# One 1024-column tile per k-step for the modulation matmuls of a two-layer decoder step, and the first normalised input in two halves

## The chip, the cores and the metric

The kernel runs on one core of a Trainium2 chip. The metric is the device time of one execution in microseconds (us). Everything is float32; the weights of the large products are split into a high and a low part (fp32r) and multiplied in three passes.

## The reference, cut to what matters

A two-layer decoder step over 512 prompt tokens and 8 x 4 sample tokens, width 1024. Each layer has a mixer and a ConvFFN, and each of these is wrapped in RMSNorms whose shift, scale and gate come from a condition vector `c` by one product per layer:

```python
c_act = jax.nn.silu(c)                      # 1 prompt row + 8 sample rows = 9 rows of 1024
for l in range(DEPTH):
    mod = (c_act @ w["ada_w"][l] + w["ada_b"][l])[:, None, :]     # 1024 -> 6144
    sh1, sc1, g1, sh2, sc2, g2 = jnp.split(mod, 6, axis=-1)
    h = _rmsnorm(x, ng[0]) * (1 + sc1) + sh1
    y, ... = _mixer_ab(h, ...) if l % 2 == 0 else _mixer_cd(h, ...)
    x = x + g1 * _rmsnorm(y, ng[1])
    h = _rmsnorm(x, ng[2]) * (1 + sc2) + sh2
    y, ... = _conv_ffn(h, ...)
    x = x + g2 * _rmsnorm(y, ng[3])
```

`ada_w` is 2 x 1024 x 6144 in float32, 50 MB of the 208 MB that the kernel moves. It is used for nine rows only.

## The kernel before

Activations lie feature-major: 128 features on the partitions, 8 k-blocks, two halves `h` of 272 tokens (256 prompt, 16 sample). A large product (`gemm`, `mm`, L527 to L531) takes one 128-column block of weights at a time: per k-block three matmuls for each half, 272 columns each. Weights come in `wraw` tiles of 256 KB (`load_w`), ScalarE makes the high part (L510), VectorE or GpSimd the low part (L511).

The order of each engine's instructions is fixed when the kernel is built, by a planner that goes through the program in order, models the time of each instruction and puts on each engine's list whatever is ready by its model; an earlier line of the program goes first. On the chip an engine then keeps to its list. SyncE (SP) issues all DMAs, also in the order of its list, and waits there when the buffer of the next DMA isn't free.

**The modulation product.** `ada(l, s)` makes 2048 of the 6144 columns of layer `l`. Stationary is `cact`, 128 x 32 (nine columns of it used), so a matmul uses a quarter of TensorE's columns, and four of them go to the four quarters of one PSUM bank:

```python
for k in range(KB):
    for j in range(4):
        wt = ada_tile()                                   # 128 x 512, 256 KB
        SY.dma_start(wt, t["ada_w"][l, k, :, o:o + 512])
        PE.matmul(ps[32*j:32*j+32, :], cact[:, k, :], wt, start=(k == 0), stop=(k == KB - 1))
    yield
```

Then ScalarE copies the bank out (L407), four 128-column transposes turn it (L410), and VectorE adds the bias and makes `mod`, `cA` (scale) and `cG` (gate). There are six calls, so 48 k-steps, 192 DMAs and 192 matmuls. In the trace a float32 matmul has two records.

**Where it runs.** `ada(0,0)` is the prologue: nothing of the network can start before it. `ada(0,1)` and `ada(0,2)` are woven into mixer 0 and `ada(1,*)` into the first ConvFFN: after each block of the gemm `weave` steps a side generator, and `pace(7, 8)` or `slow(2)` sets how many blocks go by for one k-step. The tiles come from `wraw` (7 buffers) in the prologue, from a pool `st0` (6) in mixer 0, and from pools of 4 later.

**The first input.** In the prologue `xprep` squares the input X (L458), sums it over the features on TensorE (`rstd`, L442) and multiplies by the result (L1224); `first` applies scale and shift (L1233 to L1239) once `ada(0,0)` is complete. Half 0 and half of half 1 are prepared in the prologue, the rest in `second()`, after the first half of the three lead blocks of mixer 0's gemm.

Of the kernel before, what the change touches and what calls it, by code (L numbers as in the profile page):

```python
# [41 lines left out]
XRB = 6  # L42
# [225 lines left out]
def build(nc, tc, ctx, t):  # L268
# [14 lines left out]
    def psum1(name="p1"):  # L283
        return pp.tile([P, 512], F32, name=name, tag="p1", bufs=3)
# [5 lines left out]
    cst = cp.tile([P, NCST], F32, name="cst")  # L290
    cact = cp.tile([P, KB, 32], F32, name="cact")
# [97 lines left out]
    apool = []  # L389
# [7 lines left out]
    def ada(l, s):  # L397
        ps = psum1("psada")
        for k in range(KB):
            for j in range(4):  # L400
# [7 lines left out]
        pt = psum1("psadat")  # L408
# [3 lines left out]
        V.tensor_tensor(  # L412
            mods[l][:, s * 16:s * 16 + 16, :].rearrange("p (j c) n -> p j c n", c=4),
            pt.rearrange("p (c j n) -> p j c n", c=4, j=4)[:, :, :, 0:NMOD],
            par[:, o:o + 16].rearrange("p (j c) -> p j c", c=4).unsqueeze(3).to_broadcast([P, 4, 4, NMOD]),
            op=ADD)

        def ng(i):
            oo = PAR["norm_g"][0] + (l * 4 + i) * KB
            return par[:, oo:oo + KB].unsqueeze(2).to_broadcast([P, KB, NMOD])  # L420

        mb = mods[l]
        if s == 0:
            V.scalar_tensor_tensor(cA[l][0], mb[:, 8:16, :], 1.0, ng(0), op0=ADD, op1=M)
        elif s == 1:
            V.tensor_tensor(cG[l][0], mb[:, 16:24, :], ng(1), op=M)
        else:
            V.scalar_tensor_tensor(cA[l][1], mb[:, 32:40, :], 1.0, ng(2), op0=ADD, op1=M)
            V.tensor_tensor(cG[l][1], mb[:, 40:48, :], ng(3), op=M)
        yield  # L430
# [73 lines left out]
    def load_w(ap, kc, eng):  # L504
# [3 lines left out]
        n = kc * P  # L508
        SY.dma_start(raw[:, :n], ap.rearrange("p k n -> p (k n)"))
        A.activation(hi[:, :n], raw[:, :n], AF.Copy)  # L510
        eng.tensor_tensor(lo[:, :n], raw[:, :n], hi[:, :n], op=SUB)  # L511
        return hi, lo

    def load_block(w, n, k0, k1, eng):
        out = []
        for a in range(k0, k1, 4):
            b = min(a + 4, k1)
            hi, lo = load_w(w[n, :, a:b, :], b - a, eng[a // 4 % 2])
            out += [(hi[:, i * P:(i + 1) * P], lo[:, i * P:(i + 1) * P]) for i in range(b - a)]
        return out  # L520
# [97 lines left out]
    def ffn(l, nxt, side, pre):  # L618
# [11 lines left out]
        if l == 0:  # L630
            apool.append((fp, 4))
# [42 lines left out]
        def body():  # L674
# [10 lines left out]
            apool.clear()  # L685
# [8 lines left out]
    def mixer0(nxt, side, pre, loaded):  # L694
# [5 lines left out]
        apool.append((st0, XRB))  # L700
# [84 lines left out]
        apool[-1] = (es.enter_context(pool("mix0w")), 4)  # L785
# [5 lines left out]
        apool.clear()  # L791
# [398 lines left out]
    def bias_vectors():  # L1190

        rel = ada_tile()[0:64, 0:12]
        SY.dma_start(rel, t["rel"])
        for c in range(3):
            oh, rv = ada_tile()[0:64, :], ada_tile()[0:12, :]
# [17 lines left out]
    er = ExitStack()  # L1213
    st0 = er.enter_context(pool("mix0r", side="right"))
    XR = {}

    def xprep(h, c0, c1):

        if c0 == 0:
            XR[h] = rstd(squares(h), onesD)  # L1220
        r = XR[h].unsqueeze(1).to_broadcast([P, CH, HT])
        for c in range(c0, c1, CH):
            XR[h, c] = st0.tile([P, CH, HT], F32, name="xr", tag="adaw", bufs=XRB)
            V.tensor_tensor(XR[h, c], X[:, c:c + CH, h, :], r, op=M)  # L1224
# [16 lines left out]
    a = ada(0, 0)  # L1241
# [3 lines left out]
    steps(a, 1)  # L1245
    ao, io = PAR["a_w"][0], CST["flip"][0]
    SY.dma_start(par[:, :ao], t["par"][:, :ao])
    SY.dma_start(cst[:, :io], t["cst"][:, :io])
    steps(a, 1)
    xprep(0, 0, KB)  # L1250
    steps(a, 1)
    xprep(1, 0, CH * (XRB - 4))
# [35 lines left out]
```

## Time and profile before

| | us |
|---|---|
| median of 3 runs | 1499.38 (1497.99 to 1500.75) |
| the profiled execution | 1496.03 |
| its span | 1494.3 |
| TensorE busy | 1417.8 (95%) |
| VectorE / ScalarE / GpSimd busy | 882.1 / 618.8 / 170.6 |
| mean granted TensorE clock | 0.978 of full speed |

All times within the execution are counted from the start of the span. A granted clock of 1.00 is 2.4 GHz and 0.50 is 1.2 GHz; a value between them in a row is a mean over a stretch with both. What a stretch of TensorE work costs is read from start to start of neighbouring instructions, since the ends of pipelined matmuls are modelled and overlap the next start.

### The profile page before, as it was taken

How to read it: one execution, taken by the hardware profiler on the slowest of the kernel's cores; microseconds unless marked ns; L12 is line 12 of the kernel's file. 1: busy time of each engine (PE TensorE's matmuls, PEld its weight loads, DVE VectorE, ACT ScalarE, POOL GpSimd, SP SyncE). 2: the span in 40 equal slices, each digit the busy share in tenths (PEclk: the TensorE clock that was granted, in tenths of full speed). 3: DMA queues.
4: the chain of work that ended last, by engine and by line, in shares of the span. 5: the costliest groups of instructions: out<-in, count | busy, mean ns of one | idle time of the engine just before them, and what ended most of it. 6: DMA issues, size and time to landing. Idle time of an engine off the chain costs nothing.

```text
span 1494.3 us, 26853 instructions
## 1 busy us (share of the span) xinstructions
PE 1417.8 (95%) x10354; PEld 1271.0 (85%) x10354; DVE 882.1 (59%) x1788; ACT 618.8 (41%) x1145; POOL 170.6 (11%) x384
## 2 busy tenths in 40 slices
PE   6899997999999999999799999999699999999995
PEld 2578897988798798899699999678599999999995
DVE  1664427753165346446859979652886456456457
ACT  2322235743244234235652442643674444244244
POOL 0210014110011001001500000000521011011011
PEclk9799998999999999999999999999899999999998
DMA  7775633325445546544236245446122332332311
GB/s 264 242 253 187 201 106 100 103 98 180 160 155 194 161 139 212 165 158 186 89 113 197 94 141 178 135 146 239 57 85 69 103 93 71 104 91 65 113 51 61
DMA packets 112633, 207.72 MB, mean 139 GB/s; under 512 B 20884, under 2 KB 33684, under 8 KB 111992
## 3 DMA queue, kind: packets, MB, share of 16 engines
q1 hardware_dynamic: 112504, 206.00, 42.5%
q8 instruction: 81, 1.33, 0.4%
q14 instruction: 48, 0.39, 0.1%
HBM read 198.63 MB, written 34.39 MB: 156 GB/s over the span
## 4 chain that ended last, share of the span: by engine, by line
PE 88%; DVE 6%; DMA 2%; ACT 2%; issue 1%; SPq 0%; POOL 0%; POOLq 0%; DVEq 0%; ACTq 0%
PE psmm L527 23%; PE psmm L531 23%; PE psmm L529 23%; PE psada L404 6%; PE psn L442 2%; PE psmh L529 2%; PE psmh L527 2%; PE psmh L531 2%; PE pso L1013 1%; PE psl L979 1%; PE psl L981 1%; DVE X L492 1%; DVE Yf L491 1%; DVE Y L491 1%; DVE Hlo L481 1%
## 5 line engine op out<-in xcount | busy, mean ns | idle before, releaser
L510 ACT ACTIVATE whi<-wraw 128x512 fp32r<-128x512 f32 (+1 forms) x404 | 239.8, 600 | 511.4 <-PE psmm L529 411.6
L527 PE MATMUL psmm<-Hhi,whi 128*128 128x272 f32 x2028 | 435.9, 291 | 1.0 <-DVE extu L750 1.0
L531 PE MATMUL psmm<-Hhi,wlo 128*128 128x272 f32 x2028 | 431.4, 289 | 0.3 <-POOL wlo L511 0.3
L529 PE MATMUL psmm<-Hlo,whi 128*128 128x272 f32 x2028 | 430.0, 288 | 0.0
L511 DVE TENSOR_TENSOR wlo<-wraw,whi 128x512 fp32r<-128x512 f32 (+1 forms) x374 | 240.8, 649 | 303.4 <-ACT whi L510 288.3
L527 PEld LDWEIGHTS psmm<-Hhi,whi 128*128 128x128 f32 x2028 | 321.4, 189 | 24.3 <-issue 12.6
L529 PEld LDWEIGHTS psmm<-Hlo,whi 128*128 128x128 f32 x2028 | 322.5, 189 | 9.0 <-issue 9.0
L531 PEld LDWEIGHTS psmm<-Hhi,wlo 128*128 128x128 f32 x2028 | 321.5, 189 | 9.9 <-issue 9.2
L527 PE MATMUL psmm<-act_hi,whi 128*128 128x272 f32 x624 | 135.5, 290 | 0.0
L531 PE MATMUL psmm<-act_hi,wlo 128*128 128x272 f32 x624 | 135.3, 289 | 0.0
L529 PE MATMUL psmm<-act_lo,whi 128*128 128x272 f32 x624 | 132.7, 288 | 0.0
L578 DVE SCALAR_TENSOR_TENSOR fz<-fext,par,fz 128x560 f32<-128x560 f32 x88 | 70.5, 801 | 74.3 <-ACT fz L577 74.2
L404 PE MATMUL psada<-adaw,cact 128*32 128x512 f32 x384 | 102.6, 628 | 8.3 <-DMA adaw<-ada_w 8.3
L527 PEld LDWEIGHTS psmm<-act_hi,whi 128*128 128x128 f32 x624 | 99.6, 188 | 11.8 <-issue 8.4
L531 PEld LDWEIGHTS psmm<-act_hi,wlo 128*128 128x128 f32 x624 | 99.6, 188 | 7.6 <-issue 7.5
L529 PEld LDWEIGHTS psmm<-act_lo,whi 128*128 128x128 f32 x624 | 99.1, 188 | 0.8 <-issue 0.8
L577 ACT ACTIVATE fz<-fext,par 128x560 f32<-128x560 f32 x88 | 75.2, 855 | 34.5 <-DVE fext L647 34.5
L874 DVE SCALAR_TENSOR_TENSOR zd<-extd,par,zd 128x512 f32<-128x512 f32 x120 | 87.0, 746 | 0.7
L569 POOL COPY fso<-fext 128x2 f32<-128x2 f32 x88 | 23.1, 263 | 530.6 <-ACT fext L646 530.6
L579 DVE SCALAR_TENSOR_TENSOR fz<-fext,par,fz 128x560 f32<-128x560 f32 x88 | 70.5, 801 | 2.7
L646 ACT ACTIVATE fext<-psmm 128x512 f32<-128x512 f32 (+1 forms) x88 | 49.7, 564 | 51.1 <-PE psmm L531 51.1
L527 PE MATMUL psmh<-Hhi,whi 128*128 128x272 f32 x148 | 48.2, 326 | 16.1 <-ACT Hhi L479 14.5
(260 smaller groups left out, 1692.9 us busy)
## 6 DMA issues: line engine op xcount, KB each, us to landing
adaw<-ada_w SPq DMA_DIRECT2D x192, 256.0 KB, 3.6
wraw<-w_up SPq DMA_DIRECT2D x176, 256.0 KB, 3.0
wraw<-w_dn SPq DMA_DIRECT2D x64, 256.0 KB, 2.8
o_c<-cache SPq DMA_DIRECT2D x8, 2040.0 KB, 10.0
wraw<-w_cdi SPq DMA_DIRECT2D x52, 256.0 KB, 4.6
wraw<-w_abi SPq DMA_DIRECT2D x32, 256.0 KB, 4.5
o_c<-cache SPq DMA_DIRECT2D x8, 1016.0 KB, 7.1
kc<-kc SPq DMA_DIRECT2D x28, 256.0 KB, 3.7
```

The costliest lines, as they stand in the source:

```text
L404: PE.matmul(ps[32 * j:32 * j + 32, :], cact[:, k, :], wt, start=(k == 0), stop=(k == KB - 1))
L442: PE.matmul(ps, ones, a, start=(i == 0), stop=(i == n - 1))
L510: A.activation(hi[:, :n], raw[:, :n], AF.Copy)
L511: eng.tensor_tensor(lo[:, :n], raw[:, :n], hi[:, :n], op=SUB)
L527: PE.matmul(ps[:, h, :HT], whi, xhi[:, h, :], start=(i == 0), stop=False)
L529: PE.matmul(ps[:, h, :HT], whi, xlo[:, h, :], start=False, stop=False)
L531: PE.matmul(ps[:, h, :HT], wlo, xhi[:, h, :], start=False, stop=(i == last))
L577: A.activation(z[:, :n], ext[:, 2:2 + n], AF.Identity, bias=b, scale=w[:, 2:3])
L578: V.scalar_tensor_tensor(z[:, :n], ext[:, 1:1 + n], w[:, 1:2], z[:, :n], op0=M, op1=ADD)
L579: V.scalar_tensor_tensor(z[:, :n], ext[:, 0:n], w[:, 0:1], z[:, :n], op0=M, op1=ADD)
L646: A.activation(fpr(ext, 2, h0, h1), cpr(ps, h0, h1), AF.Copy)
L874: V.scalar_tensor_tensor(cpr(z), ip, dw[:, i:i + 1], cpr(z), op0=M, op1=ADD)
```

## The change

`ada(l, s)` now goes in two passes `q`. A pass makes 1024 columns: two runs of 512 columns, 1024 columns apart. One k-step of a pass is one DMA of 512 KB into one tile of 2 x 512 columns, followed by four matmuls of 256 columns, one for each quarter. There are 96 k-steps and 96 DMAs; the matmuls are 384 of 256 columns in place of 192 of 512. After each pass its own evacuation (`ada_out`: 128 x 256), two small matmuls with a selection matrix in place of four transposes, and the bias, scale and gate of half of the k-blocks.

The tiles have a pool of their own from the start: 3 buffers of 512 KB in the prologue and mixer 0's first gemm, 2 later; `wraw` is left to weights, to the evacuated bank and to `bias_vectors`. In the side generators two k-steps in the prologue and mixer 0, one in the ConvFFN, go by for a yield, with `pace(3, 4)`. The prologue computes the statistics of both halves of X, prepares half 0, and leaves all of half 1's preparation to the point after the lead blocks' first half.

```diff
-XRB = 6
+ADB = (3, 2)
...
     def ada_tile():
-        if apool:
-            ap, n = apool[-1]
-            return ap.tile([P, CH, HT], F32, name="adaw", bufs=n).rearrange("p a n -> p (a n)")[:, 0:512]
-        return wp.tile([P, 512], F32, name="adaw", tag="wraw", bufs=WRAW)
+        return apool[-1].tile([P, 2, 512], F32, name="adaw", bufs=ADB[len(apool) - 1])
...
+        src = t["ada_w"][l].rearrange("k p (s a q n) -> s q k p a n", s=3, a=2, q=2)
+        for q in range(2):
+            ps = psum1("psada")[:, 0:256]
+            for k in range(KB):
                 wt = ada_tile()
-                o = s * 2048 + j * 512
-                SY.dma_start(wt, t["ada_w"][l, k, :, o:o + 512])
-                PE.matmul(ps[32 * j:32 * j + 32, :], cact[:, k, :], wt, start=(k == 0), stop=(k == KB - 1))
-            yield
+                SY.dma_start(wt, src[s, q, k])
+                for j in range(4):
+                    PE.matmul(ps[32 * j:32 * j + 32, :], cact[:, k, :], wt[:, j // 2, 256 * (j % 2):256 * (j % 2) + 256],
+                              start=(k == 0), stop=(k == KB - 1))
+                if k == KB - 1:
+                    ada_out(l, s, q, ps)
+                if k % per == per - 1:
+                    yield
...
-        ev = np_.tile([P, 512], F32, name="adaev", tag="nsq", bufs=NSQ)
+        ev = wp.tile([P, 256], F32, name="adaev", tag="wraw", bufs=WRAW)
...
-        for c in range(4):
-            PE.transpose(pt[:, c * P:(c + 1) * P], ev[:, c * P:(c + 1) * P], ident)
+        for c in range(2):
+            PE.matmul(pt[:, :, c, :], ev[:, c * P:c * P + P], ssel, start=True, stop=True)
...
-    def xprep(h, c0, c1):
+    def xstat(h):
+        XR[h] = rstd(squares(h), onesD)
+    def xprep(h):
...
-            XR[h, c] = st0.tile([P, CH, HT], F32, name="xr", tag="adaw", bufs=XRB)
+            XR[h, c] = np_.tile([P, CH, HT], F32, name="xr", tag="nsq", bufs=NSQ)
...
-    a = ada(0, 0)
+    a = ada(0, 0, 2)
...
-    def second():
-        k = CH * (XRB - 4)
-        first(1, 0, k)
-        xprep(1, k, KB)
-        first(1, k, KB)
...
-    pre = mixer0((0, 1), chain(delay(1), pace(chain(ada(0, 1), ada(0, 2)), 7, 8)),
-                 second, loaded)
-    pre = ffn(0, (1, 0), chain(delay(8), bias_vectors(), slow(chain(ada(1, 0), ada(1, 1), ada(1, 2)), 2)), pre)
+    pre = mixer0((0, 1), chain(delay(1), pace(chain(ada(0, 1, 2), ada(0, 2, 2)), 3, 4)),
+                 lambda: (xprep(1), first(1, 0, KB)), loaded)
+    pre = ffn(0, (1, 0), chain(delay(8), bias_vectors(), pace(chain(ada(1, 0, 1), ada(1, 1, 1), ada(1, 2, 1)), 3, 4)), pre)
```

## Rows read from the trace of the kernel before

**Rows 1.** The page: busy time of the engines, and the chain that ended last, by line.

```profile
PE 1417.8 (95%) x10354; PEld 1271.0 (85%) x10354; DVE 882.1 (59%) x1788; ACT 618.8 (41%) x1145; POOL 170.6 (11%) x384
...
PE psmm L527 23%; PE psmm L531 23%; PE psmm L529 23%; PE psada L404 6%; PE psn L442 2%; PE psmh L529 2%; PE psmh L527 2%; PE psmh L531 2%; PE pso L1013 1%; PE psl L979 1%; PE psl L981 1%; DVE X L492 1%; DVE Yf L491 1%; DVE Y L491 1%; DVE Hl
```

**Rows 2.** Busy time by stretch: stretch, its length, each engine, TensorE clock, DMA.

```profile
61.00:88.00 27.00, 27.00 (x149) 15.71 (x147) 18.47 (x52) 8.68 (x18) 3.03 (x7) 1.00 0.70 232
330.00:640.00 310.00, 310.00 (x2215) 261.46 (x2214) 141.26 (x263) 105.14 (x173) 21.04 (x82) 1.00 0.53 176
```

**Rows 3.** TensorE in order of time: start, length, line, records, around a modulation k-step.

```profile
429.72 0.41 PE L531 MATMUL psmm<-Hhi,wlo 128*128 128x272 f32 x2
430.06 1.07 PE L404 MATMUL psada<-adaw,cact 128*32 128x512 f32 x8
431.05 0.52 PE L527 MATMUL psmm<-Hhi,whi 128*128 128x272 f32 x2
431.41 0.41 PE L529 MATMUL psmm<-Hlo,whi 128*128 128x272 f32 x2
```

**Rows 4.** TensorE in order of time, around four quarter matmuls of 256 columns.

```profile
1024.42 1.07 PE L1157 MATMUL psr<-vc,sPT 128*32 128x256 f32 x16
...
1027.80 0.41 PE L527 MATMUL psmm<-Hhi,whi 128*128 128x272 f32 x2
1028.14 0.64 PE L1157 MATMUL psr<-vc,sPT 128*32 128x256 f32 x8
1028.70 0.52 PE L529 MATMUL psmm<-Hlo,whi 128*128 128x272 f32 x2
1029.06 0.41 PE L531 MATMUL psmm<-Hhi,wlo 128*128 128x272 f32 x2
```

**Rows 5.** TensorE in time: first and last modulation run in mixer 0, then in the ConvFFN.

```profile
61.35 1.06 PE L404 MATMUL psada<-adaw,cact 128*32 128x512 f32 x6
...
192.72 1.04 PE L404 MATMUL psada<-adaw,cact 128*32 128x512 f32 x2
...
330.57 1.36 PE L404 MATMUL psada<-adaw,cact 128*32 128x512 f32 x4
...
637.13 1.07 PE L404 MATMUL psada<-adaw,cact 128*32 128x512 f32 x8
```

**Rows 6.** TensorE in order of time: transposes of an evacuated bank; small float32 matmuls.

```profile
647.24 0.60 PE L410 MATMUL psadat<-cst,adaev 128*128 128x128 f32 x4
...
951.79 3.07 PE L1067 MATMUL pssm<-ks,qs 128*128 128x32 f32 x24
```

**Rows 7.** Busy time by stretch, the prologue; the last three columns are clock, DMA share, GB/s.

```profile
0.00:44.50 44.50, 31.91 (x96) 9.46 (x96) 6.96 (x15) 9.98 (x16) 2.95 (x11) 0.92 0.80 271
...
15.00:20.00 5.00, 5.00 (x17) 1.89 (x18) 0.00 (x0) 0.00 (x0) 0.00 (x0) 1.00 1.09 377
20.00:25.00 5.00, 3.38 (x12) 1.12 (x10) 2.52 (x5) 2.67 (x5) 0.00 (x0) 1.00 0.66 233
25.00:30.00 5.00, 5.00 (x17) 2.31 (x16) 1.44 (x3) 0.00 (x0) 0.00 (x0) 1.00 0.52 163
30.00:35.00 5.00, 2.72 (x18) 0.80 (x16) 2.68 (x5) 0.49 (x1) 0.00 (x0) 1.00 0.50 159
35.00:40.00 5.00, 3.07 (x6) 0.68 (x8) 0.00 (x0) 1.26 (x2) 2.48 (x2) 0.61 0.96 337
```

**Rows 8.** Waits of SyncE's queue in the first 50 us: total, times, longest.

```profile
SPq L403 <- PE psada L404: 18.2, 14, 4.0
```

**Rows 9.** VectorE and ScalarE in order of time: half 0's preparation and its scaling.

```profile
23.80 2.63 DVE L1224 TENSOR_TENSOR xr<-X,nr 128x544 f32<-128x544 f32 x4
...
46.57 4.05 ACT L1233 ACTIVATE Hhi<-xr,mod,cA 128x256 fp32r<-128x256 f32 x8 [1.36 <-DVE cA L424]
```

**Rows 10.** TensorE in order of time: the lead blocks at the low and at the full clock.

```profile
57.30 0.43 PE L531 MATMUL psmm<-Hhi,wlo 128*128 128x272 f32 x1
57.53 0.43 PE L527 MATMUL psmm<-Hhi,whi 128*128 128x272 f32 x1
...
60.63 0.29 PE L529 MATMUL psmm<-Hlo,whi 128*128 128x272 f32 x1
60.76 0.29 PE L531 MATMUL psmm<-Hhi,wlo 128*128 128x272 f32 x1
```

More of the change, by code (lines that the diff above doesn't have):

```diff
@@ L290, in build @@
     cst = cp.tile([P, NCST], F32, name="cst")
+    er = ExitStack()
+    st0 = er.enter_context(pool("mix0r", side="right"))
     cact = cp.tile([P, KB, 32], F32, name="cact")
@@ L386, in bmod @@
         return m[:, k0:k1, 1 + 4 * h:5 + 4 * h].unsqueeze(3).to_broadcast([P, k1 - k0, 4, 4])
-    apool = []
+    ssel = cp.tile([P, 4, NMOD], F32, name="ssel")
+    apool = [st0]
     def ada_tile():
-        if apool:
-            ap, n = apool[-1]
-            return ap.tile([P, CH, HT], F32, name="adaw", bufs=n).rearrange("p a n -> p (a n)")[:, 0:512]
-        return wp.tile([P, 512], F32, name="adaw", tag="wraw", bufs=WRAW)
[L397 to L400, printed above, removed]
-                wt = ada_tile()
-                o = s * 2048 + j * 512
-                SY.dma_start(wt, t["ada_w"][l, k, :, o:o + 512])
-                PE.matmul(ps[32 * j:32 * j + 32, :], cact[:, k, :], wt, start=(k == 0), stop=(k == KB - 1))
-            yield
-        ev = np_.tile([P, 512], F32, name="adaev", tag="nsq", bufs=NSQ)
+        return apool[-1].tile([P, 2, 512], F32, name="adaw", bufs=ADB[len(apool) - 1])
@@ L418, in ng @@
         def ng(i):
-            oo = PAR["norm_g"][0] + (l * 4 + i) * KB
-            return par[:, oo:oo + KB].unsqueeze(2).to_broadcast([P, KB, NMOD])
-        mb = mods[l]
+            oo = PAR["norm_g"][0] + (l * 4 + i) * KB + 4 * q
+            return par[:, oo:oo + 4].unsqueeze(2).to_broadcast([P, 4, NMOD])
+        d = slice(4 * q, 4 * q + 4)
         if s == 0:
-            V.scalar_tensor_tensor(cA[l][0], mb[:, 8:16, :], 1.0, ng(0), op0=ADD, op1=M)
+            V.scalar_tensor_tensor(cA[l][0][:, d], mb[:, 1], 1.0, ng(0), op0=ADD, op1=M)
@@ L425, in ada @@
         elif s == 1:
-            V.tensor_tensor(cG[l][0], mb[:, 16:24, :], ng(1), op=M)
+            V.tensor_tensor(cG[l][0][:, d], mb[:, 0], ng(1), op=M)
         else:
-            V.scalar_tensor_tensor(cA[l][1], mb[:, 32:40, :], 1.0, ng(2), op0=ADD, op1=M)
-            V.tensor_tensor(cG[l][1], mb[:, 40:48, :], ng(3), op=M)
-        yield
+            V.scalar_tensor_tensor(cA[l][1][:, d], mb[:, 0], 1.0, ng(2), op0=ADD, op1=M)
+            V.tensor_tensor(cG[l][1][:, d], mb[:, 1], ng(3), op=M)
@@ L507, in load_w @@
         lo = wp.tile([P, 512], F32R, name="wlo", tag="wlo", bufs=WSLOTS)
-        n = kc * P
-        SY.dma_start(raw[:, :n], ap.rearrange("p k n -> p (k n)"))
+        n = ap.shape[1]
+        SY.dma_start(raw[:, :n], ap)
         A.activation(hi[:, :n], raw[:, :n], AF.Copy)
@@ L1190, in bias_vectors, with raw @@
     def bias_vectors():
-        rel = ada_tile()[0:64, 0:12]
+        def raw():
+            return wp.tile([P, 512], F32, name="bv", tag="wraw", bufs=WRAW)
+        rel = raw()[0:64, 0:12]
         SY.dma_start(rel, t["rel"])
         for c in range(3):
-            oh, rv = ada_tile()[0:64, :], ada_tile()[0:12, :]
+            oh, rv = raw()[0:64, :], raw()[0:12, :]
             SY.dma_start(oh, t["ohp"][:, c * 512:(c + 1) * 512])
@@ L1212, in build @@
     warm(cact[:, 0, 0:1])
-    er = ExitStack()
-    st0 = er.enter_context(pool("mix0r", side="right"))
     XR = {}
-    def xprep(h, c0, c1):
[L1219 to L1222, printed above, removed]
-            XR[h, c] = st0.tile([P, CH, HT], F32, name="xr", tag="adaw", bufs=XRB)
+    def xstat(h):
+        XR[h] = rstd(squares(h), onesD)
+    def xprep(h):
+        r = XR.pop(h).unsqueeze(1).to_broadcast([P, CH, HT])
+        for c in range(0, KB, CH):
+            XR[h, c] = np_.tile([P, CH, HT], F32, name="xr", tag="nsq", bufs=NSQ)
             V.tensor_tensor(XR[h, c], X[:, c:c + CH, h, :], r, op=M)
@@ L1248, in build @@
     SY.dma_start(cst[:, :io], t["cst"][:, :io])
+    steps(a, 2)
+    xstat(0)
     steps(a, 1)
-    xprep(0, 0, KB)
-    steps(a, 1)
-    xprep(1, 0, CH * (XRB - 4))
+    xstat(1)
+    xprep(0)
     loaded = [load_block(t["w_abi"], ABI[i], 0, KB, (G, G)) for i in range(PRE)]
```

28 lines of the change are left out of this document (14 added, 14 removed).

## Prediction

> **What bounds the kernel now.** I read the page first. TensorE is busy for 95% of the span, and 6% of the chain that ended last, some 90 us, is the modulation matmuls [rows 1]. So the question is what one such matmul costs where TensorE never rests, and what the prologue costs where it does.
>
> The windows by stage answer the first half. From 330 to 640 us TensorE is busy for all 310 us, with VectorE below half and the DMA engines at 0.53 [rows 2]: time taken from TensorE there comes off the end, one for one. From 61 to 88 us the same holds, with VectorE at 18.5 of 27 us.
>
> Next I read TensorE in order of time. Around one k-step the neighbours are pairs of gemm records 0.25 us apart. Undisturbed, the second pair after the one at 429.72 would start at 430.22; it starts at 431.41 [rows 3]. The k-step costs 1.19 us. It has 8 records, that is four matmuls, and the four overlap: a run of 2 records takes 1.04, of 6 takes 1.06 and of 8 takes 1.07 us [rows 5]. So what is paid for is a run, not a matmul. The program has 40 k-steps after the prologue, but I count 26 runs from 61 to 193 us and 49 from 330 to 637 us (the first and the last of each stretch are shown) [rows 5], 75 in all, because the four DMAs of a k-step arrive at different times and the planner puts gemm matmuls between. As a check: of the 2215 records of 330 to 640 us some 192 are modulation; the other 2023 at 0.125 us make 252.9 us, and the 57.1 us left are 1.17 for each of 49 runs.
>
> In the prologue something else binds. Up to 44.5 us, when the last modulation matmul ends, the DMA engines move 12.1 MB at a mean of 271 GB/s, but the rate isn't even: 377 GB/s at 15 to 20 us, then 233, 163 and 159, then 337 [rows 7]. In the weak stretch SP stands and waits for TensorE to free modulation tiles, 18.2 us in all [rows 8].
>
> **The steady stages, part by part.** After the change each k-step waits for one DMA, so its four matmuls become ready together and I expect one run for each. Their number is 32 in mixer 0 and 48 in the ConvFFN, 80. The price of a run of four 128x32 matmuls with 256 columns stands in the trace, at another line with the same shape: the second gemm pair after the one at 1027.80 would start at 1028.30 undisturbed and starts at 1029.06, a cost of 0.76 us [rows 4]. So 75 x 1.18 = 88.5 us becomes 80 x 0.76 = 60.8 us, a gain of 27.7 us. If in mixer 0, where two k-steps go by per yield, the two always fall together, 16 records cost 1.19 (1.00 from start to start, by the row at 1024.42, and 0.19 for the gemm around it): 48 x 0.76 + 16 x 1.19 = 55.5 us and a gain of 33.0. I take 27.7, as two DMAs land apart, and keep 33.0 as the bound.
>
> The evacuation happens twelve times in place of six, ten of them in these stages. Four transposes take 0.60 us. Two float32 matmuls with 36 columns are not in the trace; the nearest are 24 records of 32 columns in 3.07 us, 0.13 each, so 0.5 us for four [rows 6]. That is 10 x 0.5 less 5 x 0.6: 2 us lost, on the path. The copies and additions on ScalarE and VectorE lie under a TensorE that is the bound; uncovered they would cost some 0.5 us each. They replace larger ones, and I count nothing. SP issues half as many DMAs. Its waits for a tile hold up the weight loads queued behind, as today, and the buffers in the pools after the prologue are 1.0 to 1.5 MB as before; TensorE waits for no weight from 61 to 640 us, so I count nothing for that either.
>
> **The prologue.** The same bytes must land. 12.1 MB at the 337 GB/s of the last stretch would take 35.8 us, 8.7 less than now. Against it: three tiles in flight are 1.5 MB where seven were 1.75; if the rate goes with them it is 289 GB/s, 41.8 us and a gain of 2.7. The interleaving that caused the weak stretch shrinks, since a k-step is one short run, but its place in TensorE's list is the planner's and may stay. I take 5.5, near the middle, and 0 to 8.7 as bounds.
>
> Making the scale and shift in halves lets `first` begin on k-blocks 0 to 3 while the second pass loads; eight ScalarE steps for half 0 take 4.05 us [rows 9], so up to 2 us and some gemm work move into DMA time. I take 1 us, with 0 and 3 as bounds. Moved the other way: four multiplications of half 1 in place of two come after the lead's first half, 2 x 0.66 = 1.3 us of VectorE [rows 9]. VectorE has room there [rows 2] and TensorE has modulation runs to do meanwhile: nothing, with 1.3 us as the bound. `second()`'s chain is what the second half of the lead blocks waits for, so this is what is late next if that cover is gone. Weights no longer share their buffers with modulation tiles and can be split earlier; that may give back part of the low-clock stretch (below), at most 3 us.
>
> **The sum.** -27.7 + 2.0 - 5.5 - 1.0 = -32.2 us. Made against the profiled execution, 1496.03, this gives 1463.8; the median of the runs shown lies 3.35 us above that execution, so I predict 1499.38 - 32.2 = 1467.2, rounded to 1467. Best bounds: -33.0 + 2.0 - 8.7 - 3.0 - 3.0 = -45.7, 1454. Worst: -27.7 + 2.0 + 1.3 = -24.4, 1475.
>
> **Rivals.**
>
> *The clock stays low through the lead.* With short runs between DMA waits TensorE rests more in the prologue. When the k-steps of 35 to 40 us waited on DMAs, the granted clock's mean fell to 0.61 [rows 7], between the levels 2.4 and 1.2 GHz, and around 57 us the lead ran at 0.23 us a matmul where 0.125 is the rate at the full clock [rows 10]. I count some 30 of the lead's 144 matmuls (three blocks, two halves, eight k-blocks, three passes) that are that slow today. If all were, 114 x 0.1 = 11 us are added: 1478. Against it: at 15 to 35 us the clock held at 1.00 through much waiting, and the modulation runs of the lead don't stop. The Trainium skill has this as a rule (TensorE: Matmul & The Clock Gate, HAM oscillation): a loop whose work per k-step is shorter than the wait for the next slice is throttled again at every step. By that rule the sum would be 1478; the trace agrees at 35 to 40 us and not at 15 to 35.
>
> *A run of 256 columns costs what one of 512 costs.* Then the change doesn't do what it says: 80 x 1.18 = 94.4 us, 5.9 more than now, and with the evacuations (2.0) and the prologue (-6.5) the total is +1.4: 1501, within the noise. For it: 2 and 8 records cost the same, so cost doesn't follow the count of columns over all matmuls. Against it: the runs of 0.76 at the same shape.
>
> *The four don't stay in a row (the slower end).* If the planner puts a gemm matmul between the four of a k-step, each split adds a run of 0.76 us. All 80 split once would add 61 us: 1528. It decides from 32.2 / 0.76 = 42 splits on. For it: half of today's k-steps are split. Against it: today's splits follow DMAs that land apart, and the groups of four that share one tile in [rows 4] are whole.
>
> **How the numbers follow.** The forecast as worked out, with ends 1454 and 1475, has 0.72; the low clock 0.14; an unchanged price per run 0.06; splits 0.08, of which half stay short of the point where it is slower. The range 1452 to 1481 holds the first, most of the second and some of the fourth. A difference of 0.2%, 3 us, is about what a measurement of this kernel can tell from none. Faster: 0.72 + 0.14 + 0.04 = 0.90. Same: 0.04, slower: 0.06, from the second and third rivals.
>
> **What would show it.** In the changed profile: 80 runs of 8 records after the prologue (or fewer with 16), each moving the gemm by 0.76 us; 330 to 640 us holding some 20 us more of the network; the last modulation matmul of the prologue near 39 us with no stretch of the DMA engines at half share; the lead's matmuls 0.125 us apart. The prediction is wrong if gemm records stand inside the groups of four, if TensorE waits for `adaw` after the prologue, or if VectorE's work on half 1 becomes what TensorE waits for.

## The result, and the profile after

The change made the kernel slower: a median of 1537.88 us (1532.83 to 1542.26, 4 runs) against 1498.97 (4 runs), a ratio of 1.0257 [1.0224, 1.0290]. I had predicted 1467. The profiled execution took 1537.81 us with a span of 1536.0.

First the page of the changed kernel: busy time, and the chain that ended last, by engine and by line.

```profile
PE 1410.8 (92%) x10762; PEld 1301.6 (85%) x10762; DVE 887.4 (58%) x1803; ACT 623.1 (41%) x1151; POOL 162.7 (11%) x384
...
PE 82%; DMA 7%; DVE 6%; ACT 3%; issue 1%; SPq 1%; POOL 0%; POOLq 0%; DVEq 0%; ACTq 0%
PE psmm L535 22%; PE psmm L537 22%; PE psmm L539 22%; PE psn L450 3%; PE psada L407 2%; PE psmh L539 2%; PE psmh L537 2%; DMA wraw<-w_dn 2%; PE psmh L535 2%; PE pso L1020 1%; DMA wraw<-w_up 1%; DMA wraw<-w_abi 1%; PE psl L986 1%; PE psl L988 1%; DMA adaw<-ada_w 1%
```

The modulation matmuls (`psada`) fell from 6% to 2% of the chain, as meant [rows 1]. In their place stand DMAs: weights (`w_dn`, `w_up`, `w_abi`) and the modulation tiles themselves. The windows of [rows 2], again with each engine, clock, DMA share and GB/s, say where:

```profile
61.00:88.00 27.00, 24.21 (x188) 19.45 (x187) 14.23 (x32) 6.22 (x12) 2.44 (x7) 0.87 0.72 243
330.00:640.00 310.00, 295.93 (x2380) 276.05 (x2379) 153.17 (x290) 114.35 (x190) 21.98 (x93) 0.97 0.55 189
```

TensorE rests for 14 us of a stretch in which it never rested, and its clock is no longer 1.00 there. What it waits for from 61 to 740 us, by its waits (total, times, longest):

```profile
PE psmm L535 <- ACT whi L518: 28.0, 11, 5.7
PE psada L407 <- DMA adaw<-ada_w: 11.9, 6, 3.5
PE psadat L421 <- ACT adaev L418: 5.2, 10, 0.6
```

and the two longest waits of SyncE's queue from 61 to 640 us:

```profile
SPq L405 <- PE psada L407: 262.6, 45, 18.5
SPq L1210 <- ACT bv L1209: 64.0, 3, 41.0
```

The first line of SyncE is the wait for a free modulation tile; the kernel before has the same wait there, not much shorter, and TensorE waited for no weight:

```profile
SPq L403 <- PE psada L404: 225.6, 66, 22.4
```

So it matters less how long SyncE stands than what stands behind it and how much was issued ahead. The second line of the changed kernel is a store of `bias_vectors`, which waits until ScalarE has made what it stores. The weights that TensorE misses (`whi`) are queued behind both.

To place the loss I numbered the gemm's matmul records in order of time (9,024 in each kernel) and set the start of the n-th against its start in the kernel before. The table is worked out from the timelines of TensorE, in us; minus is ahead of the kernel before. The other columns are experiments that come below.

```
n      before at  after   b_bv    e_bv   e_depth3  e_d343  e_noload
0           47.5     +0.2    +2.9    -1.6     +0.5     -2.6     -2.0
300        112.8     -5.3    +2.9    -8.1     -5.1     -7.6     -9.7
900        204.0     -8.7    +2.9   -11.7     -8.6    -11.1    -16.5
1050       222.7     +4.2    +2.9    +0.4     +1.9     -7.0    -16.5
1350       283.2     +2.5    +2.6    -0.8     -0.1     -6.8    -16.6
1500       304.2    +24.2   +24.0    +0.4    +21.4     -5.5    -17.7
3750       645.0    +15.7   +22.5   -14.2     +4.2    -21.7    -46.0
4050       682.8    +25.7   +22.5    -5.2    +14.1    -16.1    -40.9
4200       702.1    +37.5   +22.6    +6.3    +23.2     -4.5    -40.8
8700      1435.8    +42.0   +30.0    +9.2    +28.8     -1.0    -38.7
```

Until n = 900 the changed kernel is ahead. It loses 12.9 us by 1050 (end of mixer 0), 21.7 from 1350 to 1500 (the bias vectors), and 11.8 from 4050 to 4200 (the last down projection of the ConvFFN). Through the ConvFFN's k-steps it gains nothing: 8.5 us come by n = 3750 and 10.0 go again by 4050.

**Place one, 196 to 205 us.** SyncE in order of time (start, length, line, what, how many; the length reaches over its waits):

```profile
175.20 0.76 SPq L1217 DMA_DIRECT2D o_c<-cache  x1
197.53 0.88 SPq L405 DMA_DIRECT2D adaw<-ada_w  x2
...
199.03 11.00 SPq L517 DMA_DIRECT2D wraw<-w_abo  x10
```

From 176 to 197.5 us SyncE issues nothing: the next item on its list is a modulation tile, and no buffer is free until TensorE's run at 196.83 us. Ten weight loads stand behind it. TensorE then stands still:

```profile
196.83 1.07 PE L407 MATMUL psada<-adaw,cact 128*32 128x256 f32 x16
...
201.39 0.64 PE L407 MATMUL psada<-adaw,cact 128*32 128x256 f32 x8 [3.49 <-DMA adaw<-ada_w]
```

**Place two, 252 to 326 us**, SyncE and then TensorE:

```profile
251.25 1.18 SPq L1217 DMA_DIRECT2D o_c<-cache  x2
293.56 0.39 SPq L1210 DMA_DIRECT2D rvd<-bv  x1
294.05 0.85 SPq L517 DMA_DIRECT2D wraw<-w_up  x2
294.99 0.50 SPq L1206 DMA_DIRECT2D bv<-ohp  x1
```

```profile
291.00 1.02 PE L1208 MATMUL psrv<-bv 64*12 64x512 f32 x2
297.70 0.82 PE L535 MATMUL psmm<-Hhi,whi 128*128 128x272 f32 x2 [5.68 <-ACT whi L518]
...
311.76 0.82 PE L535 MATMUL psmm<-Hhi,whi 128*128 128x272 f32 x2 [5.28 <-ACT whi L518]
```

SyncE stands for 41 us at the store of the first bias vector. Only two weight loads follow before the next one, so TensorE waits 5.68 us for a weight behind the first vector's matmul, 5.28 behind the second's and 4.16 behind the third's.

**Place three, 693 to 735 us**, SyncE and then a window of all engines:

```profile
692.66 26.74 SPq L405 DMA_DIRECT2D adaw<-ada_w  x4
719.75 0.36 SPq L691 DMA_DIRECT2D o_f<-fso  x1
720.19 3.67 SPq L517 DMA_DIRECT2D wraw<-w_dn  x6
```

```profile
730.00:735.00 5.00, 3.49 (x14) 2.94 (x14) 3.30 (x7) 3.85 (x9) 0.00 (x0) 0.50 0.23 68
```

Each stop costs more than its wait. In the middle of the ConvFFN, TensorE in order of time:

```profile
385.70 0.41 PE L537 MATMUL psmm<-act_lo,whi 128*128 128x272 f32 x2
385.95 0.41 PE L539 MATMUL psmm<-act_hi,wlo 128*128 128x272 f32 x2
...
393.49 0.82 PE L535 MATMUL psmm<-act_hi,whi 128*128 128x272 f32 x2 [4.85 <-ACT whi L518]
...
394.56 0.65 PE L539 MATMUL psmm<-act_hi,wlo 128*128 128x272 f32 x2
395.02 0.66 PE L535 MATMUL psmm<-act_hi,whi 128*128 128x272 f32 x2
```

Before the stop a pair of records starts every 0.25 us; after a wait of 4.85 us it starts every 0.45 until 396.4 us, and the granted clock was 0.50 from 393 to 396 us. Over the whole stretch with the loss, in the changed kernel and in the kernel before:

```profile
61.00:740.00 679.00, 623.34 (x4860) 571.87 (x4859) 326.19 (x640) 240.98 (x428) 58.23 (x170) 0.94 0.51 172
61.00:740.00 679.00, 659.46 (x4729) 574.87 (x4728) 357.27 (x717) 263.65 (x483) 87.08 (x192) 0.99 0.48 159
```

As an estimate from the two mean clocks, 0.94 and 0.99, and the two levels, TensorE was at 0.50 for some 80 us in place of some 15, which can make up to some 30 us of the loss.

### The profile page after: what moved, and what is told of

Same layout as the page of the kernel before. It is cut to its first block, busy times and chain, and to the rows that moved or that the text cites. A ratio compares the mean times of both kernels' runs of the same rounds, so it can differ in the third digit from the quotient of the medians.

```text
span 1536.0 us, 27487 instructions
## 1 busy us (share of the span) xinstructions
PE 1410.8 (92%) x10762; PEld 1301.6 (85%) x10762; DVE 887.4 (58%) x1803; ACT 623.1 (41%) x1151; POOL 162.7 (11%) x384
## 4 chain that ended last, share of the span: by engine, by line
PE 82%; DMA 7%; DVE 6%; ACT 3%; issue 1%; SPq 1%; POOL 0%; POOLq 0%; DVEq 0%; ACTq 0%
PE psmm L535 22%; PE psmm L537 22%; PE psmm L539 22%; PE psn L450 3%; PE psada L407 2%; PE psmh L539 2%; PE psmh L537 2%; DMA wraw<-w_dn 2%; PE psmh L535 2%; PE pso L1020 1%; DMA wraw<-w_up 1%; DMA wraw<-w_abi 1%; PE psl L986 1%; PE psl L988 1%; DMA adaw<-ada_w 1%
## 5 line engine op out<-in xcount | busy, mean ns | idle before, releaser
L535 PE MATMUL psmm<-Hhi,whi 128*128 128x272 f32 x2028 | 441.0, 294 | 19.0 <-ACT whi L518 18.9
L537 PE MATMUL psmm<-Hlo,whi 128*128 128x272 f32 x2028 | 434.9, 291 | 0.0
L535 PEld LDWEIGHTS psmm<-Hhi,whi 128*128 128x128 f32 x2028 | 327.6, 192 | 37.7 <-ACT whi L518 25.2
L539 PEld LDWEIGHTS psmm<-Hhi,wlo 128*128 128x128 f32 x2028 | 327.4, 191 | 5.4 <-issue 2.5
L537 PEld LDWEIGHTS psmm<-Hlo,whi 128*128 128x128 f32 x2028 | 326.9, 191 | 2.3 <-issue 2.2
L407 PE MATMUL psada<-adaw,cact 128*32 128x256 f32 x768 | 65.7, 425 | 28.5 <-DMA adaw<-ada_w 28.5
L577 POOL COPY fso<-fext 128x2 f32<-128x2 f32 x88 | 21.7, 247 | 560.9 <-ACT fext L654 560.9
L407 PEld LDWEIGHTS psada<-adaw,cact 128*32 128x32 f32 x768 | 17.1, 113 | 52.5 <-DMA adaw<-ada_w 33.2
```

Of the source, the lines that this page charges most:

```text
L407: PE.matmul(ps[32 * j:32 * j + 32, :], cact[:, k, :], wt[:, j // 2, 256 * (j % 2):256 * (j % 2) + 256], start=(k == 0), stop=(k == KB - 1))
L535: PE.matmul(ps[:, h, :HT], whi, xhi[:, h, :], start=(i == 0), stop=False)
L537: PE.matmul(ps[:, h, :HT], whi, xlo[:, h, :], start=False, stop=False)
L539: PE.matmul(ps[:, h, :HT], wlo, xhi[:, h, :], start=False, stop=(i == last))
```

## The experiments

The kernel before ran beside each. "Theory S", or the theory of SyncE's list, is that loads and stores waiting in that list keep weights back.

| run | what | median us | ratio to before |
|---|---|---|---|
| changed kernel | | 1537.88 | 1.0257 [1.0224, 1.0290] |
| b_bv | before, bias vectors in the weight buffers | 1525.80 | 1.0170 [1.0147, 1.0193] |
| e_bv | changed, bias vectors in buffers of their own | 1506.70 | 1.0040 [1.0022, 1.0058] |
| e_depth3 | changed, three tiles in the later pools | 1525.34 | 1.0164 [1.0139, 1.0188] |
| e_noload | e_bv without modulation loads after the prologue | 1457.85 | 0.9724 [0.9703, 0.9745] |
| e_small | e_bv with loads of 64 KB | 1521.93 | 1.0141 [1.0110, 1.0171] |
| e_pool | changed, loads on GpSimd's queue | 1581.14 | 1.0547 [1.0526, 1.0568] |
| e_pace | changed, a k-step at each block of the ConvFFN | 1544.05 | 1.0290 [1.0274, 1.0305] |
| e_delay3 | e_bv, ConvFFN k-steps begin five blocks earlier | 1523.94 | 1.0164 [1.0126, 1.0201] |
| e_mixw4 | e_bv, four tiles late in mixer 0 | 1502.09 | 1.0016 [1.0002, 1.0031] |
| e_ffn3 | three tiles in the ConvFFN, shared with the vectors | 1502.85 | 1.0024 [1.0008, 1.0039] |
| e_d343 | both of these | 1494.94 | 0.9973 [0.9957, 0.9989] |
| e_hybrid | new in mixer 0, old k-steps in the ConvFFN | 1495.84 | 0.9972 [0.9958, 0.9986] |
| e_of | e_d343, a store behind the last loads | 1496.34 | 0.9972 [0.9959, 0.9986] |
| b_of | before, the same store moved | 1502.97 | 1.0019 [1.0007, 1.0031] |
| e_pace78 | e_d343, denser k-steps | 1510.59 | 1.0062 [1.0044, 1.0081] |
| e_pace23 | e_d343, sparser k-steps | 1513.63 | 1.0087 [1.0072, 1.0101] |

### The bias vectors: e_bv and b_bv

```diff
-            return wp.tile([P, 512], F32, name="bv", tag="wraw", bufs=WRAW)
+            return apool[-1].tile([P, 512], F32, name="bv", tag="bv", bufs=3)
```

> The changed kernel, but the buffers of bias_vectors are three of their own (6 KB of the ConvFFN's pool) in place of three of the seven raw weight buffers. The changed kernel lost 21.7 us on the kernel before while the gemm went from its 1350th to its 1500th matmul (284 to 329 us), where SyncE's list has only two weight loads between one store of a bias vector and the next and waited up to 41 us for a store's data. Theory S (SyncE's list: weight loads stand behind DMAs that wait for TensorE or ScalarE): those 20 us come back, 1515 to 1520, and the other losses stay. Rival (bandwidth: tiles of 512 KB take the DMA engines from the weight loads): under 3 us, as no byte moves differently.

Measured: 31 us less than the changed kernel, some 10 more than expected. The table of starts has the loss at place two gone (-0.8 to +0.4) and places one and three as they were; most of the rest of the gain comes in the ConvFFN's k-steps, and its cause stays open. SyncE still stands 30.7 us at the first vector's store, but five weight loads go out ahead of it. The other way round, `b_bv` makes that one move in the kernel before:

```diff
-        rel = ada_tile()[0:64, 0:12]
+        def raw():
+            return wp.tile([P, 512], F32, name="bv", tag="wraw", bufs=WRAW)
+
+        rel = raw()[0:64, 0:12]
...
-            oh, rv = ada_tile()[0:64, :], ada_tile()[0:12, :]
+            oh, rv = raw()[0:64, :], raw()[0:12, :]
```

> The kernel before, with one part of the change alone: the buffers of bias_vectors come from the seven raw weight buffers. In SyncE's list two weight loads instead of five to ten then stand between the stores of the bias vectors. Theory S (SyncE's list): 18 to 24 us lost while the gemm goes from its 1350th to its 1500th matmul, 1518 to 1524. Rival (the loss in the changed kernel needs the 512 KB tiles): 1498 to 1502.

Measured: 25.6 us slower, a little more than expected; 21.4 of it at place two. SyncE in order of time, in `b_bv`:

```profile
251.14 1.18 SPq L1210 DMA_DIRECT2D o_c<-cache  x2
293.63 0.38 SPq L1203 DMA_DIRECT2D rvd<-bv  x1
294.14 0.84 SPq L509 DMA_DIRECT2D wraw<-w_up  x2
```

In the kernel before, by contrast, SyncE stood there too, but had issued more first; the same stretch of its queue:

```profile
245.81 0.59 SPq L1196 DMA_DIRECT2D adaw<-ohp  x1
246.49 10.99 SPq L509 DMA_DIRECT2D wraw<-w_up  x4
275.36 7.52 SPq L509 DMA_DIRECT2D wraw<-w_up  x6
290.85 0.38 SPq L1200 DMA_DIRECT2D rvd<-adaw  x1
```

Ten weight loads between the first vector's load and its store, none in `b_bv`. As I read the two lists, the planner has no buffer for weights at that point when the vectors take weight buffers, and puts the store ahead of the loads. So this one move costs two thirds (`b_bv`) to four fifths (`e_bv`) of the 39 us that the change lost, and is a cause by itself.

### The modulation loads: e_noload, e_small, e_pool

`e_noload` takes the loads after the prologue away and leaves the matmuls.

```diff
-                wt = ada_tile()
-                SY.dma_start(wt, src[s, q, k])
+                wt = cst[:, 0:512].unsqueeze(1).to_broadcast([P, 2, 512])
+                if l == 0 and s == 0:
+                    wt = ada_tile()
+                    SY.dma_start(wt, src[s, q, k])
```

> The run with own buffers for the bias vectors (1506.7), and no modulation loads after the prologue: the matmuls of the other five calls read a constant that lies on the chip, so the modulation of all but the first norm is wrong. All TensorE work stays. Theory S: without these loads in SyncE's list nothing is late, and the gain worked out in the prediction comes out: 1462 to 1472. Rival (the planner's places for the k-steps, or the clock, cost it): no more than 10 us come back, 1495 to 1505.

Measured: some 48 us less than `e_bv`, and a little below the expectation. All three places are gone from the table, and the lead grows to 41 us by n = 4050. So the loads cost about 48 us against a kernel without them. Not all of that is waiting. With nothing to wait for, 48 of the 80 k-steps run here as six whole passes:

```profile
483.26 3.66 PE L409 MATMUL psada<-cst,cact 128*32 128x256 f32 x64
```

By the method of [rows 3] such a run of 64 records costs 3.8 us, 0.47 for a k-step. In the changed kernel 48 k-steps cost an estimated 35 us (by the count in the next section), here 23. So some 12 of the 48 us are cheaper runs of `e_noload`, and some 36 are what the loads themselves cost. `e_small` asks whether that is their bytes:

```diff
-                SY.dma_start(wt, src[s, q, k])
+                n = 512 if l == 0 and s == 0 else 64
+                SY.dma_start(wt[:, :, 0:n], src[s, q, k][:, :, 0:n])
```

> The run with own buffers for the bias vectors (1506.7), where each modulation load after the prologue brings 64 KB instead of 512 KB (the first 64 of each 512 columns, read eight times by the matmuls, so the modulation of all but the first norm is wrong). Loads, waits, buffers and TensorE work are the same in number. Theory S (the loss is the waiting in SyncE's list, not the bytes): most of the 49 us that the loads cost against the run without them stays, 1490 to 1505. Rival (bandwidth and time to land): most of it goes, 1460 to 1475.

Measured: with an eighth of the bytes the loss doesn't fall, it grows by 15 us, beyond both expectations. SyncE's wait for a modulation tile is as long as with whole loads (342.9 us in `e_bv`); from 50 to 730 us in `e_small`:

```profile
SPq L406 <- PE psada L410: 348.8, 49, 19.3
```

That is against bandwidth. It doesn't say why the loss grew: the order of the lists is another one again, and I left that open. `e_pool` takes the loads out of SyncE's list:

```diff
-                SY.dma_start(wt, src[s, q, k])
+                (SY if l == 0 and s == 0 else G).dma_start(wt, src[s, q, k])
```

> The changed kernel with the modulation loads after the prologue issued from GpSimd's list in place of SyncE's. Theory S: the losses at the end of mixer 0 and of the ConvFFN and the k-steps' missing gain come back (some 40 us), the 21.7 us at the bias vectors stay: 1490 to 1500. GpSimd can be held up by the same waits, which would show at its copies of the ConvFFN's state. Rival (bandwidth): the same bytes at the same times, 1533 to 1543.

Measured: the slowest of all, a miss, and above the rival's range too. From 50 to 740 us, TensorE's waits and then GpSimd's:

```profile
PE psada L407 <- DMA adaw<-ada_w: 60.1, 28, 4.0
```

```profile
POOL adaw L405 <- PE psada L407: 230.7, 57, 15.1
POOL fso L577 <- ACT fext L654: 150.9, 29, 24.5
```

GpSimd now stands at the tiles, and stands besides at what it computes, so that the modulation tiles come late. The wait had only changed its engine.

### Depth: e_depth3, e_mixw4, e_ffn3, e_d343

```diff
-ADB = (3, 2)
+ADB = (3, 3)
```

> The changed kernel with three modulation tiles in place of two in the pools after mixer 0's first gemm. Theory S: SyncE waits less for TensorE to free a tile, so part of the 13 us at the end of mixer 0, the 12 us at the end of the first ConvFFN and the some 19 us that its k-steps don't bring come back: 1510 to 1525. Rival (bandwidth): more bytes in flight at once, no gain or a loss, 1535 to 1545.

Measured: 12.5 us less than the changed kernel, at the upper end of what I expected; place two stays, and the ConvFFN's k-steps now gain 7 us (n = 1500 to 4050) where they lost 1.5. `e_mixw4` starts from `e_bv` and gives the pool late in mixer 0 four tiles (with the ConvFFN at two):

```diff
-        apool.append(es.enter_context(pool("mix0w")))
+        apool.append((es.enter_context(pool("mix0w")), 4))
```

> The run with own buffers for the bias vectors, and four modulation tiles in place of two in the pool of mixer 0's output gemm alone. There SyncE stands from 172 to 194 us at a load that waits for a k-step of TensorE, with ten weight loads behind, and the gemm loses 12 us. Theory S: with buffers free the load goes out at once, the 12 us come back at this place and no other: 1493 to 1498. Rival (bandwidth): the four loads and the weights collide in any case, 1503 to 1508.

Measured: some 4 us less than `e_bv`, between the two expectations. Place one costs 4 us in place of 12, as the theory had it, but not all of it arrives: the lead over `e_bv` is 6.4 us at n = 1050 and 3.9 at 4050. `e_ffn3` gives the ConvFFN three tiles, with room made by letting the bias vectors use halves of a modulation tile:

```diff
-            apool.append(fp)
+            apool.append((fp, 3))
...
-        rel = raw()[0:64, 0:12]
+        rel = np_.tile([P, 12], F32, name="rel")[0:64]
...
-            oh, rv = raw()[0:64, :], raw()[0:12, :]
+            w = ada_tile()
+            oh, rv = w[0:64, 0], w[0:12, 1]
```

> The changed kernel, the bias vectors in the two halves of a modulation tile (and one small tile), so not in weight buffers, and three modulation tiles in place of two in the first ConvFFN. Theory S: against the run with own buffers for the bias vectors (1506.7) part of the 18 us lost at the end of the ConvFFN and of the 8 us at a few of its k-steps come back: 1490 to 1500. Rival (the 18 us at the end come of k-steps that are late in the program): they stay, 1500 to 1507.

Measured: 2 to 4 us less than `e_bv`, by the ratios and by the medians; the intervals of the ratios overlap, and the number is the rival's, so alone the deeper pool shows no clear effect. `e_d343` joins the two (depths 3, 4 and 3):

> The changed kernel with the bias vectors out of the weight buffers and the deeper pools of both earlier runs together (three tiles, then four, then three). Theory S: their gains add, 1496 to 1500. Rival (one wait takes the place of another): 1501 to 1506.

Measured: 1494.94 and a ratio of 0.9973, 0.27% below the kernel before, and the lowest median of those that do the whole computation (`e_hybrid` and `e_of` are level with it by the ratio).

### Pace and start: e_pace, e_delay3, e_hybrid

In `e_pace` the ConvFFN's `pace(..., 3, 4)` is left out, so that the k-steps end before the last down projection; in `e_delay3`, on `e_bv`, `delay(8)` is `delay(3)`.

> The changed kernel with one k-step of the first ConvFFN for each gemm block (59 blocks, as before the change about 65) in place of three for every four, which ran to the 75th of 88. Theory S: the last k-steps no longer stand ahead of the last down product's weights, 8 to 12 us come back, 1525 to 1530. Rival (bandwidth): the same bytes in less time, 1540 to 1550.

> The run with own buffers for the bias vectors, and the side work of the first ConvFFN begun five gemm blocks earlier (delay 3 in place of 8), so that its last k-step comes at about the 70th of 88 and not among the last down product's blocks. Theory S: the four loads that held SyncE for 27 us ahead of the last down product's weights go out earlier, some 12 to 18 us come back, 1489 to 1495. Rival (two buffers are too few wherever the k-steps are): the loss moves, 1503 to 1510.

Both missed: `e_pace` came out in its rival's range and `e_delay3` above both of its ranges. Place three costs nothing in `e_pace` (+43.7 at n = 4050, +43.8 at 4200), but the denser k-steps lose more on the way. In `e_delay3` the loss moves ahead likewise (+19.3 at 4050, where `e_bv` has -5.2). Two tiles are too few at each of the three placings. `e_hybrid` therefore keeps the new scheme in the prologue and mixer 0, with four tiles late in it, and brings back the old k-steps in the ConvFFN, `slow(2)` and four tiles of 256 KB:

```diff
-    pre = ffn(0, (1, 0), chain(delay(8), bias_vectors(), pace(chain(ada(1, 0, 1), ada(1, 1, 1), ada(1, 2, 1)), 3, 4)), pre)
+    pre = ffn(0, (1, 0), chain(delay(8), bias_vectors(), slow(chain(ada_old(1, 0), ada_old(1, 1), ada_old(1, 2)), 2)), pre)
```

> The change in the prologue and mixer 0 alone, with four tiles in the pool of mixer 0's output gemm and own buffers for the bias vectors; the first ConvFFN has the modulation matmuls of the kernel before (four loads of 256 KB, matmuls of 512 columns). Theory S: the 8 to 12 us won by mixer 0 stay less some 4 at its end, and the ConvFFN loses nothing on the kernel before: 1489 to 1495. Rival (the gain in mixer 0 is eaten later in any case): 1498 to 1503.

Measured: as fast as `e_d343`. The lead of 6 to 8 us from mixer 0 lasts through the whole ConvFFN (-7.5 at n = 1050, -6.7 at 4050, -6.6 at 4200): with the old k-steps and tiles of 256 KB no stop is added.

### The third place: e_of, b_of, e_pace78, e_pace23

`e_d343` still loses 11.6 us from n = 4050 to 4200. SyncE stood there at a store, with the last weight loads behind it:

```profile
678.04 0.36 SPq L692 DMA_DIRECT2D o_f<-fso  x1
678.53 3.62 SPq L518 DMA_DIRECT2D wraw<-w_dn  x6
```

`e_of` puts the store behind them; `b_of` does so in the kernel before.

```diff
-            SY.dma_start(t[f"o_f{l}"], so)
             yield from down(ng - 1)
+            SY.dma_start(t[f"o_f{l}"], so)
```

> The depths 3/4/3 version, with the store of the ConvFFN's state (o_f, line 692) issued after the last down projection's weight loads instead of ahead of them; nothing else in SyncE's list moves. Theory (SyncE's list holds the weights back): in the 3/4/3 run SyncE stands from about 665 to 678.0 us at that store, which waits for GpSimd, with six loads for the last down projection and eight more behind it; TensorE then waits 4.0 us for a weight and runs at half clock to 695 us, and loses 12 us between 674 and 696 us against the kernel before. With the store behind the loads that loss goes: 1494.9 to 1481-1486, ratio 0.987 to 0.991. Rival (the last loads are late because the weight buffers or the engines that split them are late, and the store only happens to stand there): the loads then wait for their buffers about as long, and the time stays at 1491-1496.

> The kernel before with the same store moved behind the last down projection's loads. There the store also holds SyncE (to 694.0 us), but six of the seven loads for the last down projection were issued ahead of it, by 670.3 us, and TensorE lost nothing there. Theory (SyncE's list): no change, 1498 to 1501. Rival (the store costs time by itself, in any kernel): 3 us or more faster.

`b_of` came out 0.19% slower, 2 us above what the theory had; the rival, which had it faster, falls too. `e_of` gained nothing: the loads go out from 663.44 us, 15 us earlier, and 11.6 us are lost from n = 4050 to 4200 as before. My theory fell here, and the rival's number held. ScalarE in order of time, in `e_of`, shows what held the weights then:

```profile
679.07 0.38 ACT L419 ACTIVATE adaev<-psada 128x256 f32<-128x256 f32 x1
682.72 0.43 ACT L608 ACTIVATE yacc<-Yf 128x272 f32<-128x272 f32 x1 [3.27 <-DVE Yf L605]
...
685.81 3.21 ACT L519 ACTIVATE whi<-wraw 128x512 fp32r<-128x512 f32 x6
```

The high parts of six weight tiles stand on ScalarE's list behind the copy of the last modulation bank and the first evacuations of `Yf`, and ScalarE waits 3.27 us for VectorE ahead of them. The list was written when the kernel was built, as I read it for loads that came late in the planner's model. So the theory of SyncE's list alone was too narrow: a late load also fixes a late place for what follows it on ScalarE. The Trainium skill (Perfetto Trace Analysis, Tensor Engine Instruction) says that ScalarE's execution queue is strictly first in, first out; this trace agrees, with 6 splits behind one wait.

The two last runs change `pace(..., 3, 4)` in `e_d343` to 7, 8 and to 2, 3. Both bring splits forward on ScalarE's list.

> The depths 3/4/3 version with seven k-steps in eight blocks of the ConvFFN in place of three in four (1.14 blocks a k-step in place of 1.33), so that the k-steps end earlier. e_of showed that SyncE's store isn't what holds the last down projection back: the loads were there by 668 us, and ScalarE made six of the eight high parts only at 685.8 us, because its list has them behind the last evacuations, the modulation bank's copy and the square of Yf. In this version ScalarE's list has five of them ahead of the last up blocks' evacuation, and no modulation load stands ahead of the loads. Theory (the lists, fixed at build, put the split late where a late k-step stands in them): the 12 us between 674 and 696 us go, and denser k-steps lose 0 to 8 us in 380 to 640 us: 1483 to 1491, ratio 0.988 to 0.994. Rival (three tiles are too few for a denser pace, as two were at one block a k-step): the loss moves ahead and the time stays at 1494 or goes over it.

> The same with two k-steps in three blocks (1.5 blocks a k-step), so that the k-steps end later, in the last down projection. In ScalarE's list seven of the eight high parts stand ahead of the last up blocks' evacuation here too, but four modulation loads stand among SyncE's loads for the last down projection. Theory (the place of the split in ScalarE's list decides, not the modulation loads' number): the 12 us go and the sparser pace loses less ahead of it: 1478 to 1488, ratio 0.986 to 0.993. Rival (modulation tiles waiting in SyncE's list next to the last loads cost the time): 1495 to 1505.

Both missed as totals. `e_pace78` loses 0.2 us from n = 4050 to 4200 where `e_d343` loses 11.6; but from n = 2700 (-4.7) to 3900 (+11.1) it loses 15.8 us where `e_d343` gains 5.6, the rival's case. Of these 12.2 lie between n = 3750 and 3900, so the third place has moved ahead rather than gone. SyncE, then TensorE, in `e_pace78`:

```profile
617.64 29.96 SPq L406 DMA_DIRECT2D adaw<-ada_w  x4
```

```profile
660.35 0.82 PE L536 MATMUL psmm<-act_hi,whi 128*128 128x272 f32 x2 [5.49 <-ACT whi L519]
```

For 30 us SyncE issues four modulation loads and nothing else; the `w_dn` loads behind them go out from 648.25 us, and TensorE waits 5.49 us for what they bring. So here it is SyncE's list again. `e_pace23` loses 11.7 us from n = 3900 to 4200 (`e_d343`: 14.1) and 20.2 more from 4200 to 4500, right behind it, more than its rival had. The stops can be moved by the pace; with three tiles of 512 KB I found no pace that has none.

## Why the prediction was wrong

**The price and number of runs: right.** From 542 us, TensorE in order of time in the changed kernel:

```profile
542.25 0.41 PE L539 MATMUL psmm<-act_hi,wlo 128*128 128x272 f32 x2
542.60 0.64 PE L407 MATMUL psada<-adaw,cact 128*32 128x256 f32 x8
543.16 0.52 PE L535 MATMUL psmm<-act_hi,whi 128*128 128x272 f32 x2
543.52 0.41 PE L537 MATMUL psmm<-act_lo,whi 128*128 128x272 f32 x2
```

By the method of [rows 3] the second pair would start at 542.75 and starts at 543.52: 0.77 us, against 0.76 by [rows 4]. After 61 us I count 68 pieces, 56 of them with 8 records and 10 with 16; the other two, of 10 and 6 records, are two k-steps of which one is split. The second and third rival are out. With a double run at 57 us, and the two odd pieces taken as two runs, 58 x 0.77 + 11 x 1.19 = 57.8 us, a gain of 30.7, between my 27.7 and my bound of 33.0. That it arrives where no load is late, `e_noload` shows only in part: it is 41 us ahead at n = 4050, but with the cheaper runs named above.

**The evacuations: mis-sized.** I had them at 2.0 us on the path and the bank's copy on ScalarE at nothing, under a busy TensorE. In the waits shown above TensorE waits for that copy (`adaev`) at each of the ten evacuations, 5.2 us that the sum doesn't have.

**The prologue's 5.5 us: fell; the halves gave more.** The last modulation matmuls start later than before (43.47 us):

```profile
45.32 1.08 PE L407 MATMUL psada<-adaw,cact 128*32 128x256 f32 x8 [2.32 <-DMA adaw<-ada_w]
```

The rate is not better either (270 GB/s to 46.4 us, [rows 7] has 271), and SyncE's wait for tiles in the first 50 us is no shorter than in [rows 8]:

```profile
SPq L405 <- PE psada L407: 20.5, 12, 4.9
```

But in the first 30 records of the lead, ahead of any modulation run of either kernel, the lag goes from +0.2 to -3.7. I put this to the halves, which I had at 1.0: in these records the kernel before waits 4.0 us in four waits for the scaled input on VectorE, the changed one not at all. Both run the greater part of them at the low clock, and how much that shifts wasn't separated. So the two terms together were -3.7 and not -6.5. The first rival's cause is there: from 35 to 50 us the granted clock was 0.50 (before: 0.61, 0.71 and 0.97 in windows of 5 us, then 0.50 from 50 to 60 us); one of the three windows:

```profile
40.00:45.00 5.00, 2.20 (x20) 0.41 (x16) 4.25 (x13) 0.00 (x0) 0.13 (x1) 0.50 0.81 265
```

But in the lead the records stood 0.125 us apart again from 52 us on, where the kernel before had 0.23 at 57 us [rows 10], so the 11 us of that rival weren't paid.

**The step that failed: "Its waits for a tile hold up the weight loads queued behind, as today ... so I count nothing for that either."** From 61 to 740 us TensorE waits 28.0 us for `whi` and 11.9 for `adaw`, and its clock falls behind the stops. Three things in the step were wrong, by my reading. That TensorE waited for no weight before said how well SyncE's list was filled then, not how much it could bear. The bytes in the pools were the same, but not their grain: with two tiles of 512 KB SyncE may issue the next load only when a whole k-step of TensorE is done, where four of 256 KB come free one by one. And TensorE, faster at the k-steps, reaches the weights sooner. No run tests the grain or the speed alone. SyncE's wait for a tile from 61 to 640 us rose only from 225.6 us to 262.6. `e_noload` against `e_bv` puts the price at about 48 us, some 36 without the cheaper runs. The Trainium skill says, in a section on GpSimd's path, that any semaphore wait of a DMA happens on the issuing sequencer ahead of the dispatch (DMA: Bandwidth & Descriptors, Anatomy of one DMA — SWDGE (gpsimd) path); the 22 and 41 us in which SyncE issued nothing agree.

**The move that I didn't cost.** I listed `bias_vectors` nowhere in the prediction, although the change moves its buffers into `wraw`. `b_bv` measures it: 26 us on its own, `e_bv` 31 in the changed kernel.

Together, the table of starts gives the distance between the changed kernel and `e_noload`, 80.7 us at the end: 12.9 at place one, 22.8 at place two, 24.7 through the ConvFFN's k-steps, 11.7 at place three, and 8.6 in small parts elsewhere; some 12 of it are the cheaper runs. As an estimate, the terms then add up to what was measured: -30.7 (runs), +2.0 as forecast and +5.2 (evacuations), -3.7 (prologue and halves), +31 (bias vectors) and +36 (loads) make +40 us, against the measured +39. In the prediction's own words, what would make it wrong was "if TensorE waits for `adaw` after the prologue"; it did, but `whi` was the longer wait.

**What stays open.** Removing the loads (`e_noload`) and the vectors' move (`e_bv`, `b_bv`) show these two as causes, and more or smaller tiles (`e_depth3`, `e_d343`, `e_hybrid`) give a part back. How much of the rest is SyncE's order at run time and how much the places that the planner gave to the splits on ScalarE was not separated, nor why `e_small` lost more.

## What to carry to other kernels

Before moving a buffer into a pool that weights use, or making a tile larger, go through the list of the engine that issues the DMAs and ask at each load or store what stands behind it: a wait there is paid by the next stage's weights, not by the load itself. "The bottleneck waits for nothing today" is no price for such an edit. Where lists are fixed at build, a later load also puts its dependents later on other engines, so an edit that only frees the queue may give nothing back; count the buffers in units of what one step frees.

## What was unexpected of the hardware

A stop of TensorE of 3 to 5 us cost more than itself: after the 4.85 us at 393.49, pairs of records started 0.45 us apart in place of 0.25 for 2.9 us; in the window from 730 to 735 us the granted clock was 0.50. Loads of an eighth of the bytes saved nothing where SyncE waited 348.8 us for their buffers (`e_small`). And a wait of SyncE has no price of its own: 34 us at the three stores of the bias vectors cost about 1 us in `e_bv`, 64 us at the same stores some 22 in the changed kernel.
